# Gate loads of the first merge group in pairs, and the order of the last scan visit's products

## The chip, the cores and the metric

The kernel runs on one core of a Trainium2 chip. A core has a matrix engine (TensorE, PE in the profile), VectorE (DVE), ScalarE (ACT), GpSimd (POOL) and SyncE (SP), which here issues the DMA transfers between the chip's memory (HBM) and the on-chip buffer (SBUF). Products of PE go to a buffer of their own, PSUM. The metric is the device time of one execution in microseconds (us); lower is better.

## The reference

One layer of a diffusion backbone over 2048 latent tokens of width 1024, with 256 context tokens as a prefix. Two bidirectional linear-attention mixers, GLA and Gated DeltaNet (GDN), run on the same normalised input. What matters here is the merge of the two at the end:

```python
def branch_merge(oa, ob, ag, bg, mg, ...):
    ya = rmsnorm(oa, gla_onorm).reshape(b, t, GLA_V) * jax.nn.silu(ag)
    yb = rmsnorm(ob, gdn_onorm).reshape(b, t, GDN_V) * jax.nn.silu(bg)
    gates = jax.nn.sigmoid(mg + b_gate.astype(jnp.float32))
    merged = gates[..., :D_MODEL] * jnp.matmul(ya, w_gla_out) + gates[..., D_MODEL:] * jnp.matmul(yb, w_gdn_out)
    return jnp.matmul(merged, w_o)
```

The layer then adds `gt_x * out` to the input and applies a final RMSNorm. The mixers scan chunk by chunk in both directions, each scan from the final state of the context in that direction.

## The kernel before

The program is unrolled Python. A framework gives each tile a buffer, sets the waits and orders the instructions of each engine; where two instructions are ready, the one that comes first in the program goes first, and a buffer that comes free goes to the earliest one waiting for its pool. `keep_in_program_order` (`pin`) fixes the order of an instruction by hand.

Three phases follow each other: `phase_proj` (input projections, convolution, the in-chunk solves of GDN), `phase_mix` (the scans) and `phase_out` (merge and output projection).

`phase_mix` has 16 visits. In each, one 128-token chunk of the forward and one of the backward direction is scanned. Several generators are woven: `weave` always advances the one whose next step, at 1/n of its length per step, comes first. In a 17th round, `si == len(order)`, the last visit's products are still to be made: `gdn_scan` for both directions (weight 12) gives the products of L1055, L1066, L1077 and L1097, and `gla_end` (weight 4) gives the GLA output products L1346 and L1354 and their adds on VectorE, L1364. Beside them the merge is begun: `out_weights` and then `out_merge(0)` (weight 10).

`out_weights` loads the raw weights of both output projections, one block of 128 columns after the other (`out_raw`, L1559, 512 KB per block), and `split` makes a high part (ScalarE, L132) and a low part (L135, on VectorE for even blocks and GpSimd for odd ones). At its first step it also splits the first group's `y` (`out_y(0)`), whose raw tiles come by `y_raw` (L1580). It yields once, after block 0.

The raw tiles, of `out_raw`, `y_raw` and later of the rows of `w_o` and other reloads, all come from one pool with four buffers of 4 KB per partition (`self.rp`, name `wr`), opened in the last visit.

`out_merge(g)` merges one group of 512 tokens; `groups` has four. For each of eight column blocks j and for the two mixers i, it loads a gate tile `ga` (L1600, 128x512, 256 KB), makes twelve matmuls (L1605: four k times high-high, high-low and low-high) into a PSUM tile, and multiplies with the gate on VectorE (L1608). The two halves are added (L1612) and stored to `d_m` (L1613). In group 0 the gates have three small buffers (`os`), and both products use `pm`, which has two PSUM tiles. The half i = 0 reads the tiles `y0` and `y2`, the half i = 1 reads `y1` and `y3`.

`phase_out` begins with `out_y(1)`: `y_raw` for the four quarters of the second group, casts and low parts, into tiles of its own. Then, for g = 1 to 3, it calls `out_y(g + 1)` for the next group's `y` and runs `out_merge(g)` with other work woven in (`prep`: rows of `w_o`; `blocks`: splits of the last factors). The transposes L1416 with L1417 and the stores L1419 belong to the finishing of scanned chunks.

Of the kernel before, what the change touches and what calls it, by code (L numbers as in the profile page):

```python
# [11 lines left out]
F32 = mybir.dt.float32  # L12
# [10 lines left out]
P = 128  # L23
# [74 lines left out]
class Build:  # L98
# [1340 lines left out]
    def phase_mix(self):  # L1439
        nc = self.nc  # L1440
# [39 lines left out]
        for si in range(len(order) + 1):  # L1480
            gens = []
            if si == NLAT // 2:
                self.act_set("natural_log_exp_and_others")
            if si == len(order) - 1:
                self.rp = self.pool("owr", 4, side="right")
                self.raws = [self.out_raw(j) for j in range(2)]
                self.yraw = [self.y_raw(self.groups[0][0], hf) for hf in range(2)]
            if si == 1:
                self.ectx.close()
                gtc = gctx.enter_context(ExitStack())  # L1490
                gt = self.gt_row(gtc)
            if si in (1, 2):
                gens.append((itertools.islice(gt, 5 if si == 1 else 6), 6))
            elif si == 3:
                gtc.close()
            if si == 0:
                for d in range(2):
                    gens.append((itertools.chain(*[self.gdn_scan(p[d][1], False) for p in pairs]), 8))
                gens.append((self.gla_ctx_states(pairs), 4))
            else:  # L1500
                pair = [x[0] for x in prev]
                self.gla_prev(pair)
                for x in prev:
                    x[1]["prev"] = self.prev_o(1, x[1]["c"] - NCTX)
                for x in prev:
                    gens.append((self.gdn_scan(x[1], True, si == len(order)), 12))
                if si == len(order):
                    gens.append((self.gla_end(pair), 4))
            cur = []
            if si < len(order):  # L1510
                for d in range(2):
                    c = order[si][d]
                    a, b = ({"kp": kps[si % 2]} for _ in range(2))
                    self.gla_load(d, c, a)
                    cur.append((a, b))
                if si == 0:
                    rest()
                for d in range(2):
                    c, a = order[si][d], cur[d][0]
                    a["v"] = a["kp"].tile([P, 512], F32, name="av")  # L1520
                    nc.sync.dma_start(a["v"], self.d_av[c])
                for d in range(2):
                    self.gdn_load(d, order[si][d], cur[d][1])
                if si == 0:
                    nc.sync.dma_start(self.am.rearrange("p l t -> p (l t)"), self.io["ki"][:, 2 * len(MASK_LEVELS) * 64:])
                gens.append((self.gla_step(*[x[0] for x in cur], pair if si else None), 24))
            else:
                gctx.close()
                self.out_open()
                gens.append((itertools.chain(self.out_weights(), self.out_merge(0)), 10))  # L1530
            self.weave(gens)
            for g in self.fin:
                next(g)
            if si == len(order):
                self.fin_rest(4)
            prev = cur
# [25 lines left out]
    def out_weights(self):  # L1562
        raws = self.raws
        for j in range(8):
            cs = slice((j % 2) * P, (j % 2) * P + P)
            if j == 0:
                self.out_y(0)
            if j < 6:
                raws.append(self.out_raw(j + 2))
            hi, lo = self.wab[j // 2]  # L1570
            self.split(hi[:, :, cs], lo[:, :, cs], raws.pop(0), lo=self.LO[j % 2])
            if j == 0:
                yield

    LO = ("vector", "gpsimd")

# [16 lines left out]
    def out_merge(self, g):  # L1593
        nc, y = self.nc, self.y2
        pin = self.tc.keep_in_program_order if g else lambda x: x
        for j in range(8):
            gs = []
            for i in range(2):
                ga = (self.sp if i else self.spa).tile([P, 512], F32, name="ga")
                nc.sync.dma_start(ga, self.d_gate[g, :, 8 * i + j, :])  # L1600
                ps = self.pv() if g and i else self.pm.tile([P, 512], F32, name="pm")
                n = 0
                for k in range(4):
                    for wi, yy in ((0, y[i]), (0, y[2 + i]), (1, y[i])):
                        nc.tensor.matmul(ps, self.wab[j // 2][wi][:, 4 * i + k, (j % 2) * P:(j % 2) * P + P],  # L1605
                                         yy[:, k, :], start=(n == 0), stop=(n == 11))
                        n += 1
                pin(nc.vector.scalar_tensor_tensor(ga, ga, 1.0, ps, op0=ALU.add, op1=ALU.mult))  # L1608
                gs.append(ga)
                if i == 0:  # L1610
                    yield
            pin(nc.vector.tensor_tensor(gs[0], gs[0], gs[1], op=ALU.add))  # L1612
            nc.sync.dma_start(self.d_m[g, :, j, :], gs[0])  # L1613
            yield
# [284 lines left out]
```

## Time and profile before

| | |
|---|---|
| median of 3 runs | 2144.94 us (2143.9 to 2147.0) |
| the profiled execution | 2138.93 us |
| its span, first to last instruction | 2136.9 us |
| granted PE clock, mean | 0.987 |
| PE busy | 2041.9 us (96%) |
| VectorE, ScalarE, GpSimd busy | 1283.2, 914.5, 816.7 us |
| first product of group 0 (L1605) | 1779.3 us from the span's start |
| last L1605 of group 3 | 1970.3 us |

The profile gives one execution. Its timeline lists instructions by engine with start, duration, engine, line, operation, output and inputs; a bracket at the end is the time for which the engine was idle before, and what ended it. "x12" is a run of twelve instructions merged into one row, and the duration is that of the run. A matmul's end is modelled, so a row's duration is a little longer than the step from one to the next. SPq is the queue in which SP issues DMAs; its rows have the time of the issue, not of the transfer. A view by windows has, for each stretch of time, the busy time of every engine, PE's granted clock, the busy share of the DMA engines and GB/s.

### The profile page before, as it was taken

How to read it: one execution, taken by the hardware profiler on the slowest of the kernel's cores; microseconds unless marked ns; L12 is line 12 of the kernel's file. 1: busy time of each engine (PE TensorE's matmuls, PEld its weight loads, DVE VectorE, ACT ScalarE, POOL GpSimd, SP SyncE). 2: the span in 40 equal slices, each digit the busy share in tenths (PEclk: the TensorE clock that was granted, in tenths of full speed). 3: DMA queues.
4: the chain of work that ended last, by engine and by line, in shares of the span. 5: the costliest groups of instructions: out<-in, count | busy, mean ns of one | idle time of the engine just before them, and what ended most of it. 6: DMA issues, size and time to landing. Idle time of an engine off the chain costs nothing.

```text
span 2136.9 us, 40356 instructions
## 1 busy us (share of the span) xinstructions
PE 2041.9 (96%) x15208; PEld 1674.4 (78%) x15208; DVE 1283.2 (60%) x2229; ACT 914.5 (43%) x2208; POOL 816.7 (38%) x746
## 2 busy tenths in 40 slices
PE   6999999999999999999999999899988888999998
PEld 2688888888888888777777777688888876787786
DVE  2713555556667653555555655466567776576776
ACT  3645245555543223444344444345545656002332
POOL 2410122222221104566666665256556656002211
PEclk9999999999999999999999999999999999999999
DMA  8323122222222224443344443688888877898543
GB/s 285 111 86 119 48 58 76 63 62 65 73 63 72 72 72 133 149 143 129 122 146 141 159 144 110 202 306 284 296 291 297 296 250 233 286 317 300 181 147 111
DMA packets 272862, 346.96 MB, mean 162 GB/s; under 512 B 25000, under 2 KB 176796, under 8 KB 272668
## 3 DMA queue, kind: packets, MB, share of 16 engines
q1 hardware_dynamic: 272668, 344.39, 48.8%
q8 instruction: 120, 1.97, 0.4%
q14 instruction: 74, 0.61, 0.1%
HBM read 218.73 MB, written 125.57 MB: 161 GB/s over the span
## 4 chain that ended last, share of the span: by engine, by line
PE 72%; DMA 7%; issue 7%; DVE 6%; ACT 5%; POOL 3%; SPq 1%; DVEq 0%; POOLq 0%; ACTq 0%
PE pz L371 46%; PE pm L1605 3%; PE pz L1605 2%; DMA g<-dg 2%; PE pe L943 1%; PE pe L1125 1%; PE pl L1002 1%; PE pl L995 1%; PE pz L1087 1%; DMA ga<-dgate 1%; PE pl L1003 1%; DVE ql L1222 1%; ACT E L1216 1%; PE pp L1823 1%; PE pz L1066 1%
## 5 line engine op out<-in xcount | busy, mean ns | idle before, releaser
L371 PE MATMUL pz<-hi,wh 128*128 128x512 f32 (+1 forms) x1560 | 621.2, 399 | 1.1 <-DVE hi L134 1.1
L371 PE MATMUL pz<-lo,wh 128*128 128x512 f32 (+1 forms) x1560 | 600.1, 385 | 1.8 <-POOL lo L135 1.8
L371 PE MATMUL pz<-hi,wl 128*128 128x512 f32 (+1 forms) x1520 | 588.1, 387 | 0.0
L371 PEld LDWEIGHTS pz<-lo,wh 128*128 128x128 f32 x1560 | 294.6, 189 | 51.2 <-POOL lo L135 3.7
L371 PEld LDWEIGHTS pz<-hi,wh 128*128 128x128 f32 x1560 | 294.1, 189 | 47.1 <-DVE hi L134 1.7
L371 PEld LDWEIGHTS pz<-hi,wl 128*128 128x128 f32 x1520 | 285.9, 188 | 53.7 <-issue 0.4
L135 POOL TENSOR_TENSOR wl<-w,wh 128x1024 fp32r<-128x1024 f32 x44 | 109.6, 2491 | 437.5 <-ACT wh L132 314.2
L575 DVE SCALAR_TENSOR_TENSOR acc<-zpad,cw,acc 128x1024 f32<-128x1024 f32 x192 | 269.5, 1403 | 6.6
L880 DVE CAST_PREDICATED U<-kit,pl 128x256 f16<-128x256 int32 x216 | 91.3, 432 | 138.7 <-PE pl L1003 135.0
L996 ACT CAST ppb<-pl 128x256 f16<-128x256 f32 x216 | 73.8, 374 | 169.9 <-PE pl L995 163.2
L1605 PE MATMUL pm<-y,wb 128*128 128x512 f32 x480 | 118.5, 399 | 5.2 <-DVE ga L1608 2.9
L1223 POOL TENSOR_TENSOR E<-E,ak 128x256 f32<-128x256 f32 x96 | 79.4, 847 | 111.5 <-ACT E L1216 67.0
L135 DVE TENSOR_TENSOR sql<-sq,sqh 128x512 fp32r<-128x512 f32 (+1 forms) x36 | 28.0, 804 | 142.7 <-ACT sqh L132 142.5
L1605 PEld LDWEIGHTS pm<-y,wb 128*128 128x128 f32 x480 | 90.9, 191 | 26.9 <-DVE y L135 2.6
L630 POOL TENSOR_TENSOR acc<-acc,sq 128x512 f32<-128x512 f32 x32 | 50.6, 1590 | 138.7 <-ACT sq L629 90.9
L560 ACT COPY zpad<-pz 128x512 f32<-128x512 f32 x48 | 28.2, 588 | 137.5 <-PE pz L371 137.5
L1125 PE MATMUL pe<-wt,gh 128*128 128x256 f32 x264 | 77.0, 320 | 8.8 <-ACT E L1216 4.9
L880 DVE CAST_PREDICATED Tm<-kit,pl 128x256 f16<-128x256 int32 x180 | 76.4, 425 | 0.0
L1002 PEld LDWEIGHTS <-Tm 128*128 128x128 f16 x864 | 55.1, 98 | 26.5 <-issue 22.0
L132 ACT CAST wh<-w 128x1024 fp32r<-128x1024 f32 x44 | 46.2, 1049 | 68.6 <-PE pz L371 56.0
L1216 ACT ACTIVATE E<-pe 128x128 f32<-128x128 f32 x320 | 64.5, 306 | 18.7 <-PE pe L1125 18.1
L1222 DVE TENSOR_TENSOR ql<-E,q 128x256 f32<-128x256 f32 x96 | 64.1, 694 | 13.6 <-ACT E L1213 11.7
(326 smaller groups left out, 4265.3 us busy)
## 6 DMA issues: line engine op xcount, KB each, us to landing
gd<-dgd SPq DMA_DIRECT2D x32, 768.0 KB, 7.8
w<-in_w_in SPq DMA_DIRECT2D x44, 512.0 KB, 3.5
dgate<-ob SPq DMA_DIRECT2D x128, 128.0 KB, 1.8
qk<-dqkv SPq DMA_DIRECT2D x32, 512.0 KB, 5.9
ga<-dgate SPq DMA_DIRECT2D x64, 256.0 KB, 4.7
x<-in_x SPq DMA_DIRECT2D x28, 512.0 KB, 5.0
dqkv<-acc SPq DMA_DIRECT2D x192, 64.0 KB, 1.6
dgd<-tm SPq DMA_DIRECT2D x36, 256.0 KB, 2.5
```

The lines of the kernel that those rows point to most:

```text
L135: getattr(nc, lo).tensor_tensor(dst_lo, src, dst_hi.bitcast(F32), op=ALU.subtract)
L371: nc.tensor.matmul(ps[:, 0:n], a[:, kk, :], b[:, kk, :], start=(k == 0), stop=(k == last - 1))
L575: nc.vector.scalar_tensor_tensor(acc, src, wcol, acc, op0=ALU.mult, op1=ALU.add)
L630: nc.gpsimd.tensor_tensor(v, v, r, op=ALU.mult)
L880: self.nc.vector.copy_predicated(out, mv, data)
L996: nc.scalar.copy(ppl, pc.rearrange("p h (j i) -> p h j i", i=m))
L1002: nc.tensor.matmul(pu[:, h], Tm[:, h], ppl[:, h], start=True, stop=True)
L1125: self.nc.tensor.matmul(out, g[:, i, ct * P:(ct + 1) * P], self.wt[:, d, cols[0]:cols[1]], start=(j == 0), stop=(j == 1))
L1216: nc.scalar.activation(E[:, ct, li, x].rearrange("p (j e i) -> p e j i", e=2, i=m), s[:, x * P:(x + 1) * P].rearrange("p (e j i) -> p e j ...
L1222: nc.vector.tensor_tensor(ql[:, li], E[:, :, li, 0], q, op=ALU.mult)
L1223: nc.gpsimd.tensor_tensor(E[:, :, li, 1], E[:, :, li, 1], k, op=ALU.mult)
L1605: nc.tensor.matmul(ps, self.wab[j // 2][wi][:, 4 * i + k, (j % 2) * P:(j % 2) * P + P], yy[:, k, :], start=(n == 0), stop=(n == 11))
```

## The change

Three edits. `gla_end` gets weight 8 in place of 4, so its steps come at 1/8, 2/8 and 3/8 of the weave and not at 1/4, 2/4 and 3/4. `out_weights` yields three times after block 0, so weight blocks 1 to 7 and the first product come at 4/10 of the weave and not at 2/10; the products of `gdn_scan` have their steps at 1/12 to 5/12. And in group 0, for the blocks j = 1 to 7, both gate tiles of a block come in one transfer of 512 KB into a tile of the pool `wr`; block 0 keeps the two small tiles, and the other groups are as before.

```diff
                 if si == len(order):
-                    gens.append((self.gla_end(pair), 4))
+                    gens.append((self.gla_end(pair), 8))
...
             if j == 0:
                 yield
+                yield
+                yield
...
         for j in range(8):
             gs = []
+            if g == 0 and j:
+                t = self.w_raw().rearrange("p (i n) -> p i n", i=2)
+                nc.sync.dma_start(t, self.d_gate[g, :, j:16:8, :])
             for i in range(2):
-                ga = (self.sp if i else self.spa).tile([P, 512], F32, name="ga")
-                nc.sync.dma_start(ga, self.d_gate[g, :, 8 * i + j, :])
+                if g == 0 and j:
+                    ga = t[:, i]
+                else:
+                    ga = (self.sp if i else self.spa).tile([P, 512], F32, name="ga")
+                    nc.sync.dma_start(ga, self.d_gate[g, :, 8 * i + j, :])
```

`w_raw` takes a tile of the pool `wr`:

```python
    def w_raw(self):
        return self.rp.tile([P, 8, P], F32, name="wr").rearrange("p a b -> p (a b)")
```

## The prediction

> **What bounds the kernel now.** I read the page first, for the share of PE, then the chain of work that ended last around the first merge group, then each engine's timeline there. I write block j for the eight column blocks of a merge group and call its two products GLA (i = 0) and GDN (i = 1).
>
> ```profile
> span 2136.9 us, 40356 instructions
> PE 2041.9 (96%) x15208; PEld 1674.4 (78%) x15208; DVE 1283.2 (60%) x2229; ACT 914.5 (43%) x2208; POOL 816.7 (38%) x746
> ```
>
> PE is busy for 96% of the span, and no edit removes a matmul. Only idle PE time or a low clock can be won. Inside the first group the chain steps through loads of the gate tile `ga`, and VectorE's timeline shows waits for them:
>
> ```profile
> 1814.20 0.69 DVE L1608 SCALAR_TENSOR_TENSOR ga<-ga,pm 128x512 f32<-128x512 f32 x1 [1.90 <-DMA ga<-dgate]
> ...
> 1829.20 0.69 DVE L1608 SCALAR_TENSOR_TENSOR ga<-ga,pm 128x512 f32<-128x512 f32 x1 [3.11 <-DMA ga<-dgate]
> ```
>
> The columns are start, duration, engine and line; the bracket is the idle time before and what ended it. VectorE waits up to 3.11 us for a gate load. What matters is PE's own timeline:
>
> ```profile
> 1774.05 2.12 PE L1077 MATMUL pz<-rhs,gd 128*128 128x128 f32 x14
> 1778.67 0.66 PE L1416 MATMUL pe<-kf,og 128*128 128x128 f32 x4 [2.49 <-POOL og L1412]
> ...
> 1779.30 0.48 PE L1605 MATMUL pm<-y,wb 128*128 128x512 f32 x1
> 1782.07 5.06 PE L1605 MATMUL pm<-y,wb 128*128 128x512 f32 x11 [2.29 <-DVE y L135]
> 1786.93 1.16 PE L1346 MATMUL pz<-av,at 128*128 128x128 f32 x8
> 1788.02 1.10 PE L1354 MATMUL pz<-Sa,q 64*64 64x128 f32 x32
> 1789.05 3.02 PE L1605 MATMUL pm<-y,wb 128*128 128x512 f32 x12
> 1791.91 1.95 PE L1097 MATMUL pz<-vn,gd 128*128 128x128 f32 x16
> 1793.61 16.87 PE L1605 MATMUL pm<-y,wb 128*128 128x512 f32 x72
> 1812.44 16.60 PE L1605 MATMUL pm<-y,wb 128*128 128x512 f32 x72 [1.96 <-DVE ga L1608]
> 1830.03 5.69 PE L1605 MATMUL pm<-y,wb 128*128 128x512 f32 x24 [0.99 <-DVE ga L1608]
> 1835.57 1.03 PE L1416 MATMUL pe<-kf,oi 128*128 128x128 f32 x8
> ...
> 1840.18 2.96 PE L1605 MATMUL pz<-y,wb 128*128 128x512 f32 x12
> ```
>
> The reader should see two separate losses. Ahead of the first product PE is idle for 2.49 us and 2.29 us, and then 11 matmuls take 5.06 us, where 72 later take 16.87, that is 0.234 us each: 2.49 us more than 11 x 0.234. Inside the group the gate loads cost PE just 1.96 + 0.99 = 2.95 us, since two PSUM tiles let it run ahead of VectorE. All of it is 4.78 + 2.49 + 2.95 = 10.2 us, or 0.48% of the span: the ceiling. About 0.2% (4.3 us) is what a measurement of this kernel can tell from no change.
>
> **The change part by part.**
>
> *Scan products ahead of the first product.* `gla_end` and the empty yields put L1346 and L1354 (1786.93 to 1789.05, about 2.1 us) and L1097 (1.78 us from 1791.91 up to 1793.61, roughly) ahead of L1605 in program order. The GLA part needs only states and the masked score tile, finished long before, so it can lie in the idle time. Nothing is added: the same instructions, no DMA. VectorE's adds behind them (L1364, L1098) move with them, past the splits of weight blocks 2 and 4; I cost that at nothing, since VectorE is busy for only 1.19 and 0.73 of 2 us from 1784 to 1788 (rows below). Without that cover it would be one add, some 0.7 us, on pair 1's load. Block 1 could then begin about 2 to 4 us sooner than 1793.61, and some of the half-clock stretch may go too. But I cost this edit by what is late next, and that is the load of block 1's gates.
>
> *Gate pairs in the weight buffers.* Seven pairs replace 14 single loads (512 KB instead of two of 256 KB; the bytes are equal; SP issues 7 fewer DMAs of some 0.4 us). Before, block 1's GLA gate was loaded at 1761.40 with block 0's two, in the third small buffer (first row below). Now the first pair needs one of four `wr` buffers, and those hold raw weights until their splits end:
>
> ```profile
> 1761.40 1.82 SPq L1600 DMA_DIRECT2D ga<-dgate  x3
> ...
> 1786.07 0.51 SPq L1559 DMA_DIRECT2D wr<-in_w_gla_out  x1
> 1790.38 1.22 DVE L135 TENSOR_TENSOR wb<-wr,wb 128x1024 fp32r<-128x1024 f32 x1
> 1791.43 2.40 POOL L135 TENSOR_TENSOR wb<-wr,wb 128x1024 fp32r<-128x1024 f32 x1 [1.16 <-ACT wb L132]
> 1794.90 1.21 DVE L135 TENSOR_TENSOR wb<-wr,wb 128x1024 fp32r<-128x1024 f32 x1
> 1796.43 2.40 POOL L135 TENSOR_TENSOR wb<-wr,wb 128x1024 fp32r<-128x1024 f32 x1 [2.61 <-ACT wb L132]
> 1791.98 1.05 ACT L132 CAST wb<-wr 128x1024 fp32r<-128x1024 f32 x1 [0.63 <-DMA wr<-in_w_gdn_out]
> ```
>
> Weight blocks 4 to 7 give their buffers back at 1790.38 + 1.22 = 1791.6, 1793.8, 1796.1 and 1798.8. A load of 512 KB took, from issue to the cast that waited for it, 1786.07 to 1791.98 = 5.9 us; a row below has 4.2. So pair 1 lands between 1795.8 and 1797.5; I take 1796.5. Block 2's first product needs the PSUM tile that VectorE frees 0.69 us later: about 1797.3. Before, it began at 1793.61 + 24 x 0.234 = 1799.2. From there pairs 2 to 7 are early by several us, both gate waits go, and PE runs 6 x 24 x 0.234 = 33.7 us to 1831.0. Before, the group ended at 1830.03 + 5.69 = 1835.7. That is a **gain of 4.7 us** (3.7 to 5.4) inside the group, for both edits together.
>
> *What this moves.* Those buffers aren't empty in the trace. They hold the raw `y` of the second group:
>
> ```profile
> 1797.97 1.74 SPq L1580 DMA_DIRECT2D wr<-dy  x4
> ...
> 1806.46 0.85 SPq L1580 DMA_DIRECT2D wr<-dy  x2
> 1810.68 1.05 ACT L132 CAST y<-wr 128x1024 fp32r<-128x1024 f32 x1 [1.67 <-DMA wr<-dy]
> 1811.80 2.38 POOL L135 TENSOR_TENSOR y<-wr,y 128x1024 fp32r<-128x1024 f32 x1 [1.19 <-ACT y L132]
> ```
>
> Here the four raw tiles load from 1797.97 on, and the last is split by 1814.2, some 21 us before group 1 needs it. In the change the seven pairs come first in program order, and each holds its buffer until its merged block is stored. Pairs 5, 6 and 7 take what blocks 1, 2 and 3 release; the four `y` loads get what blocks 4, 5, 6 and 7 release. The last waits for the end of the group. The store that it waits for, and the SP load released by it:
>
> ```profile
> 1800.08 0.69 DVE L1612 TENSOR_TENSOR ga<-ga 128x512 f32<-128x512 f32 x1
> 1800.80 0.32 SPq L1613 DMA_DIRECT2D dm<-ga  x1
> 1809.74 0.32 SPq L1613 DMA_DIRECT2D dm<-ga  x1
> 1812.05 0.32 SPq L1600 DMA_DIRECT2D ga<-dgate  x1
> 1815.64 0.32 SPq L1613 DMA_DIRECT2D dm<-ga  x1
> 1818.29 0.32 SPq L1600 DMA_DIRECT2D ga<-dgate  x1
> ```
>
> From the end of a block's last product to its store is about 1.5 us (0.69 + 0.69 and handovers); the store lands after 2.31 (1809.74 to 1812.05) or 2.65 us (1815.64 to 1818.29). I take 2.6. A `y` load took 1806.46 to 1810.68 = 4.2 us beside other traffic; with little else in flight I take 3.8, near the middle between 4.2 and 3.2 (a store's 2.31 and 0.85 of issue); the far end is the 5.9 of a weight load. Then ScalarE casts (1.05 us), and VectorE (1.22) or GpSimd (2.40) makes the low part. For the GDN half, released by block 7: 1831.0 + 1.5 + 2.6 + 3.8 + 1.05 + 2.40 = 1842.4. Group 1's second product began at 1840.18 before, so it is **2.2 us late**. For the GLA half, released by block 6 (5.6 us sooner, faster low part): 1835.6. So PE idles from 1831.0 to 1835.6, less about 2.1 us of transposes (L1416: 8 take 1.03 us in the row at 1835.57, and 16 are left) that fit in, works until 1838.4, and idles again until 1842.4. Queued behind on ScalarE and GpSimd are the casts of group 2's `y`, wanted only 45 us later: they cost nothing. On SP the weight loads for `w_o` come later by some us, with a whole group's time to spare.
>
> *The clock.* The rows of the first stage, by 2 us (the number before the DMA share is the granted clock):
>
> ```profile
> 1768.00:1770.00 2.00, 1.02 (x9) 1.02 (x10) 2.00 (x9) 1.90 (x12) 1.80 (x3) 1.00 0.03 8
> 1770.00:1772.00 2.00, 2.00 (x12) 2.00 (x11) 1.71 (x6) 1.96 (x11) 1.61 (x2) 0.52 0.00 0
> ...
> 1780.00:1782.00 2.00, 0.00 (x0) 0.00 (x0) 2.00 (x6) 1.04 (x1) 1.73 (x2) 0.58 0.69 199
> 1784.00:1786.00 2.00, 2.00 (x6) 1.60 (x5) 1.19 (x1) 0.78 (x1) 0.26 (x1) 0.50 1.11 309
> 1786.00:1788.00 2.00, 2.00 (x11) 1.62 (x9) 0.73 (x2) 1.04 (x1) 0.12 (x1) 0.72 1.12 283
> ...
> 1830.00:1832.00 2.00, 1.97 (x9) 1.67 (x10) 0.86 (x2) 0.00 (x0) 0.00 (x0) 1.00 0.28 80
> ```
>
> Full clock turns to half after two gaps of 2.49 and 2.29 us, and already once around 1770 after smaller ones. The new gaps, 2.5 and about 4 us, are longer, so I expect a fall. If it comes in the first gap, it mostly slows a product that would wait anyway: nothing. In the second it costs up to 2.5 us, as above. I take 0.8, nearer to nothing, since the first gap comes first.
>
> The Trainium skill, "TensorE: Matmul & The Clock Gate", Part 1, says that the clock is halved after an idle window of about 3.4 us that runs freely. By that alone the first gap would be harmless and the second would halve the clock only where a window falls wholly inside it. The rows around 1770 and 1780 speak against so strict a reading, since no single gap there is that long.
>
> *Sum.* 2.2 + 0.8 = +3.0 us after the second group's second product; from there on PE is busy without a gap until the next stage, so nothing absorbs it. The profiled execution took 2138.93 us; the median of the runs is 2144.94, 6.0 us more. I add the difference to the median: **2147.9 us**, +0.14%. The bounds of the unknown durations: early ends (pair 1 at 1795.8, store 2.3, load 3.2, no clock price) give 3.0 - 0.7 - 0.3 - 0.6 - 0.8 = +0.6; late ends (+1.0, +0.1, +2.1, clock +1.7) give +7.9, hardly all at once.
>
> **The rivals.**
>
> *A. Clock stays full* in the gaps. The rest as forecast: +2.2, 2147.1 us. For it: after the gap of 0.99 us that ends at 1830.03 the row at 1830 has 1.00; against it, the rows near 1780. This is the case by the strict rule of the page named above. Chance 0.13.
>
> *B. Slower: the second gap grows and halves the clock.* If `y` loads take 5.9 us, as weight loads did, the GDN half comes 2.1 us later, and a gap of 6 us surely costs the full 2.5: 2.2 + 2.1 + 2.5 = +6.8, 2151.7 us. It decides from a load of about 5 us. For it: group 1's gate loads start in the same microseconds. Against: in the row at 1830 the DMA engines are busy for 0.28 only. Chance 0.25.
>
> *C. Faster: `y` isn't held back*, because buffers are given out in another order. Then group 1 follows at once and the gain of 4.7 us stays: 2140.2 us, and up to 2 us better if the early stage also keeps full clock and pair 1 comes early. For it: `y` loads have no other cause to wait. Against: the raw loads in the trace of before stand in program order. Chance 0.17.
>
> *D. The scan products don't move* ahead in effect (PSUM tiles `pz` are three, and the scan's own products hold them). Then block 2 begins at 1799.2 as before, 2 us later than in the forecast: +5.0, 2149.9 us. Chance 0.05.
>
> **How the numbers follow.** The forecast has 0.40, and its own range is about +0.6 to +5. C is the only faster case, 0.17. Slower are B and D, 0.30. Within 0.2% are the forecast and A, 0.53. The range, 2140 to 2152 us, goes from C's value to just above B's, and leaves out the far ends of both.
>
> **What would show it.** In the changed trace: L1354 ahead of the first L1605; no wait of VectorE for gates after block 2; the last L1580 load of group 1's `y` issued only after the store (L1613) of block 7; PE idle in two places around the border of groups 0 and 1, ended by `y` low parts; and a granted clock below 1 there. I am wrong if the `y` loads are issued before 1815, or if PE goes from group 0 to group 1 without a gap.

## The result and the profile after

The changed kernel took 2162.41 us (median of five runs, 2160.95 to 2169.06) where the kernel before, timed beside it, took 2144.42 (median of six); a sixth run of the changed kernel, 7337.84 us at a mean granted clock of 0.26, is left out here and in the ratio. The ratio is 1.0097 (95% interval 1.0077 to 1.0118): about 20.8 us **slower**, outside the range that was given. All times "in us" below that come from a ratio are the ratio's excess times 2144.4.

The profiled execution has a longer span, with the same number of matmuls:

```profile
span 2164.1 us, 40346 instructions
PE 2052.4 (95%) x15208; PEld 1680.6 (78%) x15208; DVE 1289.4 (60%) x2229; ACT 913.8 (42%) x2208; POOL 820.0 (38%) x746
```

Two profiled executions differ already ahead of the change, so I count from a common mark: the last L1354 row of the scan visit before the 17th round. These are the mark, the first product of the last stage (L1823 before, L1831 after) and the product there that follows the first pass, all from PE's timeline, before:

```profile
1760.18 1.10 PE L1354 MATMUL pz<-Sa,q 64*64 64x128 f32 x32
1970.53 0.63 PE L1823 MATMUL pz<-y,hi 128*128 128x512 f32 x2
1989.63 0.70 PE L1823 MATMUL pz<-y,hi 128*128 128x512 f32 x2 [1.77 <-DVE x L1830]
```

and after, with what lies between (L1613 is the old L1605; L1616, L1620 and L1621 are the old L1608, L1612 and L1613; L1608 is the old L1600):

```profile
1764.41 1.10 PE L1354 MATMUL pz<-Sa,q 64*64 64x128 f32 x32
...
1775.50 2.08 PE L1346 MATMUL pz<-av,at 128*128 128x128 f32 x8 [1.68 <-ACT at L1252]
...
1785.86 0.47 PE L1613 MATMUL pm<-y,wb 128*128 128x512 f32 x1
1788.78 2.50 PE L1613 MATMUL pm<-y,wb 128*128 128x512 f32 x5 [2.45 <-DVE y L135]
1792.64 3.70 PE L1613 MATMUL pm<-y,wb 128*128 128x512 f32 x11
...
1807.14 30.20 PE L1613 MATMUL pm<-y,wb 128*128 128x512 f32 x132 [1.14 <-DVE wr L1616]
1839.53 3.02 PE L1613 MATMUL pm<-y,wb 128*128 128x512 f32 x12 [2.18 <-DVE wr L1616]
...
1845.80 4.38 PE L1613 MATMUL pm<-y,wb 128*128 128x512 f32 x11 [0.77 <-DVE y L135]
1851.94 2.83 PE L1613 MATMUL pz<-y,wb 128*128 128x512 f32 x11 [1.53 <-POOL y L135]
...
1880.51 4.35 PE L1613 MATMUL pm<-y,wb 128*128 128x512 f32 x12 [2.64 <-DVE ga L1616]
...
1985.36 4.61 PE L1613 MATMUL pm<-y,wb 128*128 128x512 f32 x12 [2.77 <-DVE ga L1616]
...
1992.61 0.63 PE L1831 MATMUL pz<-y,hi 128*128 128x512 f32 x2
...
1999.72 0.79 PE L1831 MATMUL pz<-y,lo 128*128 128x512 f32 x1 [3.68 <-DVE lo L1652]
...
2016.86 0.70 PE L1831 MATMUL pz<-y,hi 128*128 128x512 f32 x2 [1.93 <-DVE x L1838]
```

Measured from the mark, and with the rows of before that the prediction shows:

| point | before | after | lost so far |
|---|---|---|---|
| first product of group 0 | 19.1 | 21.5 | +2.3 |
| first product of block 2 | 39.0 | 42.7 | +3.7 |
| end of group 0 | 75.5 | 78.1 | +2.6 |
| end of group 1's second product | 83.0 | 90.4 | +7.4 |
| first product of the last stage | 210.4 | 228.2 | +17.8 |
| the product after its first pass | 229.4 | 252.4 | +23.0 |
| end of the span | 376.7 | 399.7 | +23.0 |

So four pieces: +2.6 us up to the end of group 0 (where a gain of 4.7 was forecast), +4.8 at the border, +10.4 in the rest of groups 1 to 3 (where PE was forecast to run without a gap), +5.2 in the first pass of the last stage. After that nothing moves. Of the 10.4, three gaps of PE are 6.4 (2.64, 2.77 and one of 1.00 at 1926.64) and two falls of the clock, below, 3.1. The reader should see that gaps ended by `ga` (VectorE's gate product) have appeared at 1880.51 and 1985.36, far behind the group that was edited, and one ended by `lo` at 1999.72.

**Why the first group gains nothing.** ScalarE's timeline of after has the cast of weight block 4 behind a square (L1409) that waits for a scan output, and SP's queue has the first pair only after it:

```profile
1798.05 0.31 ACT L1409 ACTIVATE fsq<-oi 128x128 bf16<-128x128 f32 x1 [5.54 <-DVE oi L1098]
...
1798.36 1.03 ACT L132 CAST wb<-wr 128x1024 fp32r<-128x1024 f32 x1
```

```profile
1801.63 0.61 SPq L1602 DMA_DIRECT2D wr<-dgate  x1
...
1826.81 0.60 SPq L1608 DMA_DIRECT2D ga<-dgate  x1
...
1837.16 2.54 SPq L1582 DMA_DIRECT2D wr<-dy  x4
1840.22 0.32 SPq L1621 DMA_DIRECT2D dm<-wr  x1
1844.39 2.22 SPq L1582 DMA_DIRECT2D wr<-dy  x5
...
1862.03 0.42 SPq L1608 DMA_DIRECT2D ga<-dgate  x1
```

The prediction gave the first `wr` buffer back at 1791.6, which is 31.4 us behind the mark; the pair was issued 37.2 us behind it. But the square is the smaller part of these 5.8 us. The load of weight block 4 was itself late, 26.9 us behind the mark where before it was 22.0. The issue of its GLA half, before and after:

```profile
1782.14 0.49 SPq L1559 DMA_DIRECT2D wr<-in_w_gla_out  x1
```

```profile
1791.28 0.41 SPq L1559 DMA_DIRECT2D wr<-in_w_gla_out  x1
```

The cast then came 5.6 us late (before it began at 1788.50). In SP's order the load stands behind a store (L1419, 1790.19) that waited for VectorE. The rows of L1582, the loads of raw `y`, stand between the stores L1621, as was forecast.

**Where the gates went.** The same rows hold a trap. SP issues a gate load at 1826.81 and the next one at 1862.03: none for 35 us. But by 1826.81 eight loads had been issued, two for block 0 and six for group 1, and its six small buffers were full; before, they were full only at 1843.4. The seventh load needs VectorE's first sum of group 1 and follows it at once (that sum ends at 1861.6). So it is VectorE that is late. Its first gate product of group 1, before:

```profile
1841.78 0.68 DVE L1608 SCALAR_TENSOR_TENSOR ga<-ga,pm 128x512 f32<-128x512 f32 x1
```

and after, behind a low part of group 2's `y` (group 1's four casts are over by 1849.5):

```profile
1857.53 2.17 DVE L135 TENSOR_TENSOR y<-wr,y 128x1024 fp32r<-128x1024 f32 x1 [4.43 <-ACT y L132]
1859.62 0.68 DVE L1616 SCALAR_TENSOR_TENSOR ga<-ga,pm 128x512 f32<-128x512 f32 x1
```

That is 81.6 and 95.2 us behind the mark, 13.6 us late, where PE's second product ends 7.4 us late. The view of waits for groups 1 to 3 (engine, line, what it waited for: total us, times, longest) has VectorE's waits for gates, before (1832 to 1992):

```profile
DVE ga L1608 <- DMA ga<-dgate: 7.3, 4, 2.5
```

and after (1840 to 2020) these, and PE's for VectorE's gate product, which before had none:

```profile
DVE ga L1616 <- DMA ga<-dgate: 35.6, 13, 5.6
...
PE pm L1613 <- DVE ga L1616: 6.4, 3, 2.8
```

Only the second of these rows is lost time: while PE runs ahead, a wait of VectorE costs nothing. The order of the weave alone (below) has 31.1 us of such waits of VectorE and 2.3 of PE's (1836 to 2020).

SP waits for VectorE's sums (to store them; 43.8 us in this window, 14.5 before), VectorE waits for gates, and the gates stand behind SP's waits: a ring in which a delay can be handed on from block to block. The start of the last stage shows one turn of it. SP's queue, then VectorE:

```profile
1988.59 4.32 SPq L1708 DMA_DIRECT2D wr<-dwoB  x2
...
1993.50 0.97 SPq L1608 DMA_DIRECT2D ga<-dgate  x2
```

```profile
1998.38 0.69 DVE L1616 SCALAR_TENSOR_TENSOR ga<-ga,pm 128x512 f32<-128x512 f32 x1 [5.27 <-DMA ga<-dgate]
1998.98 1.29 DVE L1652 TENSOR_TENSOR lo<-r,hi 128x512 fp32r<-128x512 f32 x2
```

SP is held for 4.32 us by two reloads into `wr` that wait for buffers; the last gates of group 3 are issued behind them at 1993.50; VectorE stands 5.27 us for them; `lo`, which the last stage needs, stands behind that product in VectorE's order; and PE's row at 1999.72 is idle for 3.68 us. The rest of the 5.2 us there, about 1.5, is the clock, which was 0.57 from 1999 to 2003. VectorE's order did the same inside the border: the second gate product of block 6, behind the low part of `y`, is what PE waited for in the row at 1839.53 (2.18 us):

```profile
1837.65 1.23 DVE L135 TENSOR_TENSOR y<-wr,y 128x1024 fp32r<-128x1024 f32 x1 [5.02 <-ACT y L132]
1838.79 0.68 DVE L1616 SCALAR_TENSOR_TENSOR wr<-wr,pm 128x512 f32<-128x512 f32 x1
```

**The clock** fell as feared, and again later. By windows (length, then PE's and the others' busy time, then the granted clock, DMA share and GB/s), after:

```profile
1843.00:1850.00 7.00, 5.22 (x17) 3.84 (x16) 4.40 (x6) 2.09 (x2) 1.83 (x2) 0.76 0.62 191
...
1878.00:1888.00 10.00, 7.49 (x27) 6.01 (x28) 7.26 (x11) 0.00 (x0) 0.00 (x0) 0.83 0.84 291
...
1985.00:1993.00 8.00, 7.64 (x26) 6.12 (x27) 7.62 (x10) 3.65 (x5) 3.30 (x1) 0.79 0.84 292
```

Before, it was 1.00 from 1836 to 1990. Twelve products took 4.35 and 4.61 us at 1880.51 and 1985.36, against 2.96 elsewhere.

### The profile page after: what moved, and what is told of

The parts are those of the page before. It is cut to its first block, busy times and chain, and to the rows that moved or that the text cites. A ratio compares the mean times of both kernels' runs of the same rounds, so it can differ in the third digit from the quotient of the medians.

```text
span 2164.1 us, 40346 instructions
## 1 busy us (share of the span) xinstructions
PE 2052.4 (95%) x15208; PEld 1680.6 (78%) x15208; DVE 1289.4 (60%) x2229; ACT 913.8 (42%) x2208; POOL 820.0 (38%) x746
## 4 chain that ended last, share of the span: by engine, by line
PE 67%; DMA 9%; issue 7%; DVE 7%; ACT 5%; POOL 3%; SPq 1%; DVEq 0%; POOLq 0%; ACTq 0%
PE pz L371 45%; DMA g<-dg 2%; PE pm L1613 2%; PE pe L943 1%; PE pe L1125 1%; DMA ga<-dgate 1%; PE pl L1002 1%; PE pl L995 1%; PE pl L1003 1%; PE pz L1087 1%; DVE ql L1222 1%; DVE acc L575 1%; PE pp L1831 1%; ACT E L1216 1%; DMA av<-dav 1%
## 5 line engine op out<-in xcount | busy, mean ns | idle before, releaser
L1613 PE MATMUL pm<-y,wb 128*128 128x512 f32 x480 | 123.2, 410 | 14.1 <-DVE ga L1616 6.4
L1613 PEld LDWEIGHTS pm<-y,wb 128*128 128x128 f32 x480 | 93.9, 198 | 38.0 <-DVE ga L1616 8.2
```

## The experiments

All run kernels are compared with the kernel before on the same chip. L numbers shift by a few lines between them; `ga` in a bracket (`wr` for a pair) is always the gate product and `y` a low part of `y`.

### Each edit by itself

The order of the weave alone (no pairs):

```diff
-                    gens.append((self.gla_end(pair), 4))
+                    gens.append((self.gla_end(pair), 8))
...
                 yield
+                yield
+                yield
```

> The order edit alone (gla_end weight 8, two more empty yields); gates in the three small buffers as before. Theory T (the whole loss comes from the raw y of groups 1 and 2, which wait for the weight buffers that the gate pairs hold): between 2140 and 2149 us, within 5 us of before, and no PE gap at the border of groups 0 and 1. Rival O (the new order costs it: ScalarE takes the squares of the last scan output ahead of the casts of weight blocks 4 to 7, as the changed trace shows at 1792 to 1798): 2154 us or more, over 10 us above before.

> Both halves of the order edit and no pairs, a second time with more rounds. If the halves cost only together: a ratio of 1.002 to 1.003 again. If the two are harmless as each was alone: 0.999 to 1.001, and the first run was high by chance.

Measured: 1.0024 (1.0009 to 1.0039), and the second time 1.0028 (1.0014 to 1.0042): 5 to 6 us slower, so not chance. The pairs alone, with the old order:

```diff
+            if g == 0 and j:
+                t = self.w_raw().rearrange("p (i n) -> p i n", i=2)
+                nc.sync.dma_start(t, self.d_gate[g, :, j:16:8, :])
...
-                ga = (self.sp if i else self.spa).tile([P, 512], F32, name="ga")
-                nc.sync.dma_start(ga, self.d_gate[g, :, 8 * i + j, :])
+                if g == 0 and j:
+                    ga = t[:, i]
+                else:
+                    ga = (self.sp if i else self.spa).tile([P, 512], F32, name="ga")
+                    nc.sync.dma_start(ga, self.d_gate[g, :, 8 * i + j, :])
```

> The gate pairs alone, the weave as before. Theory T: 2157 to 2166 us, 13 to 22 us above before, with y loads of group 1 issued only after stores of blocks 4 to 7 and PE gaps at the border of groups 0 and 1. Rival O: at most 8 us above before, 2152 us.

Measured: 1.0070 (1.0045 to 1.0095), 15.0 us slower. The two parts together make 20 to 21 us, the whole of it. PE's timeline of the pairs alone has the gaps of after, with the same enders:

```profile
1832.65 3.02 PE L1611 MATMUL pm<-y,wb 128*128 128x512 f32 x12 [2.59 <-DVE wr L1614]
...
1844.80 2.83 PE L1611 MATMUL pz<-y,wb 128*128 128x512 f32 x11 [1.66 <-POOL y L135]
...
1991.56 0.80 PE L1829 MATMUL pz<-y,lo 128*128 128x512 f32 x1 [5.24 <-DVE lo L1650]
```

### Is it the hold on group 1's `y`?

Three pairs only, so that one of the four buffers goes to `y` at once and the others after the pairs of blocks 1 to 3:

```diff
-            if g == 0 and j:
+            if g == 0 and 0 < j < 4:
...
-                if g == 0 and j:
+                if g == 0 and 0 < j < 4:
```

> The whole change, but pairs only for blocks 1 to 3; blocks 4 to 7 take the small buffers. The fourth weight buffer then goes to y at once, and the others after blocks 1 to 3. Theory T: 2142 to 2152 us, most of the loss gone, y loads of group 1 from about 1800 to 1820 us of the span. Rival O: still 2155 us or more.

> Pairs for blocks 1 to 3 alone, the weave as before. If pairs in the buffers that are truly empty save the gate gaps of group 0 (2.95 us) and the order edit costs 5 us: 2137 to 2142 us, 1 to 4 us below before. If e4 came out level only because pairs make the order edit harmless: 2141 to 2146 us.

Measured with the new order: 0.9996 (0.9983 to 1.0009); with the old order: 0.9988 (0.9973 to 1.0002). The cost is gone in both. But fewer pairs change the loads of group 0 as well, so a second test keeps all seven and frees `y` from the pool: group 1's raw `y` is loaded straight into the tile of its low part and split in place.

```diff
-                raw = self.yraw.pop(0) if self.yraw else self.y_raw(self.groups[g][e], hf)
+                if g != 1:
+                    raw = self.yraw.pop(0) if self.yraw else self.y_raw(self.groups[g][e], hf)
...
+                if g == 1:
+                    b = self.groups[g][e]
+                    for x in range(2):
+                        self.nc.sync.dma_start(dst[1][:, :, x].bitcast(F32), self.d_y[2 * b + x, :, 4 * hf:4 * hf + 4, :])
+                    raw = dst[1].bitcast(F32)
```

> The whole change, but the raw y of group 1 is loaded straight into its low-part tile and split in place, so it needs no weight buffer; the pairs keep all seven. If the waiting y causes all the loss that e1 (order alone) doesn't have: about 5 us above before, 2145 to 2150 us, and no PE gap at the border of groups 0 and 1. If only the border (7.6 us in the changed trace) hangs on it and the late gate loads of groups 1 to 3 have a cause of their own: 2152 to 2158 us.

> Seven pairs, the weave as before, y of group 1 loaded in place (no weight buffer). If the hold on y is all that is wrong with the pairs: 2137 to 2144 us. If the pairs cost by themselves: 2150 us or more, near e2.

Measured with the whole change: 1.0031 (1.0013 to 1.0050), 6.6 us slower in place of 20.8; with the pairs and the old order: 1.0012 (0.9991 to 1.0033), 2.6 us in place of 15.0. So the wait of group 1's `y` for `wr` buffers carries 12 to 14 us, and what is left in the first is about the order edit's 5 to 6. Without the wait, the first product of the last stage comes at 212.0 us from the mark (the mark is at 1763.20 in that run; 210.4 before, 228.2 after), so most of the loss in groups 1 to 3 went too, though only the source of that `y` was changed: it is a consequence of that wait. VectorE's waits for gates stayed; it is PE's waits for VectorE that nearly went (1836 to 2020):

```profile
DVE ga L1622 <- DMA ga<-dgate: 33.3, 14, 6.3
...
PE pm L1619 <- DVE ga L1622: 1.9, 2, 1.2
```

VectorE's first gate product of group 1 begins at 82.5 us from the mark in this run, nearly as early as before.

### What hands the delay on

First I held that group 2's `y`, whose low parts VectorE makes in the middle of group 1's gate products, was what delayed the gates. So group 2's `y` was asked for five steps later:

```diff
-                    y = self.y2
-                    self.out_y(g + 1)
-                    nxt, self.y2 = self.y2, y
...
-                for _ in gen:
+                for n, _ in enumerate(gen):
+                    if g < 3 and n == (5 if g == 1 else 0):
+                        self.out_y(g + 1)
+                        nxt = self.y2
```

> The whole change, but the y of group 2 is asked for only after five steps of group 1's merge, so that its low parts don't stand ahead of group 1's gate products on VectorE. If the waits on VectorE behind group 2's y carry the second part of the loss (all that comes after group 1's second product, about 15 us in the changed trace): 2148 to 2156 us. If the loss after the border comes from late gate loads of another cause, or from the border alone: within 3 us of the change, 2160 to 2167 us.

Measured: 1.0105 (1.0081 to 1.0128). Nothing was won, so what the theory forecast **failed**. But the run doesn't refute it, since the edit put another hold in place of the first. VectorE's first gate product of group 1 was on time (80.2 us from the mark, which is at 1764.86 there). Now group 2's `y` loads, the last at 1869.43, stood in SP's queue just ahead of the gates, whose next loads came 105.5 us from the mark (before 86.5, after 97.6):

```profile
1870.35 1.37 SPq L1608 DMA_DIRECT2D ga<-dgate  x3
```

The run also shows that late loads of `w_o` aren't needed for the loss: they were issued 76.9 us from the mark there, near 75.2 before, and not 91.6 as in after. The next suspect was SP's order, where gate loads stand behind stores that wait for VectorE. The stores of groups 1 to 3 were moved to GpSimd's queue:

```diff
-            nc.sync.dma_start(self.d_m[g, :, j, :], gs[0])
+            (nc.gpsimd if g else nc.sync).dma_start(self.d_m[g, :, j, :], gs[0])
```

> The whole change, but the merged blocks of groups 1 to 3 are stored from GpSimd's queue, so that SP's queue has no store ahead of a gate load. The border stays as in the change. If gate loads in groups 1 to 3 are late because they stand behind stores in SP's queue: 5 to 12 us below the change, 2150 to 2158 us, and VectorE's waits for gates fall from 35.6 us to under 15. If they are late for their buffers or for DMA: within 3 us of the change, 2160 us or more.

Measured: 1.0067 (1.0043 to 1.0090), 14.4 us slower, so about 6.4 of the 20.8 are won back, though the two intervals overlap by a little (1.0077 to 1.0090). VectorE's waits for gates fall to these (under 15 was expected), in the same view and the window 1836 to 2020:

```profile
DVE ga L1616 <- DMA ga<-dgate: 22.5, 11, 5.2
```

Inside groups 1 to 3 one gap is left, 1.21 us, where after had 2.64, 1.00 and 2.77; the border's gaps, which the stores don't cause, remain, and so does `lo` (3.70 us); one of 2.21 us for a cast is new at the start of the last stage. So the stores in SP's order carry a part of the delay, clearly in PE's gaps and less surely in the time. How the rest is shared between VectorE's order and SP's stays open. For the reloads in SP's order (the row at 1988.59) no run of its own was made: that part is read from the trace.

### What is dear in the order edit

> Only the part of the weave edit that raises the weight of the last scan products (gla_end 8), without the two empty steps ahead of block 3's and block 4's weight casts. Theory (the empty steps cost: ScalarE's casts of blocks 4 to 7 fall behind the squares of the last scan output, so the gate gaps of group 0 grow from 2.95 us to 6): 2139 to 2144 us, within 2 us of before, and the gate gaps of group 0 stay at 2 to 4 us. Rival (the moved scan products themselves cost): 2145 us or more, with the gaps of the first experiment.

> Only the two empty steps, without the raised weight of the scan products. Theory (the empty steps cost): 2145 to 2149 us, gate gaps in group 0 of 5 to 6 us. Rival (the moved scan products cost): 2140 to 2144 us, gaps near 3 us.

The raised weight alone measured 0.9990 (0.9974 to 1.0006), the empty steps alone 1.0008 (0.9996 to 1.0020). My theory, that the empty steps cost because they put ScalarE's casts behind the squares, **fell** too. They do put the cast of block 4 there, as ScalarE's timeline of the empty steps alone shows:

```profile
1786.46 0.31 ACT L1409 ACTIVATE fsq<-oi 128x128 bf16<-128x128 f32 x1 [2.01 <-DVE oi L1098]
...
1786.77 1.03 ACT L132 CAST wb<-wr 128x1024 fp32r<-128x1024 f32 x1
```

The raised weight alone does it to the cast of block 5 (before, it was block 7's). Either costs nothing that can be measured: without pairs no gate load needs the buffers that those splits free. With pairs one does:

```diff
-                    gens.append((self.gla_end(pair), 4))
+                    gens.append((self.gla_end(pair), 8))
```

> All seven pairs and the raised weight, without the empty steps. If the empty steps make the whole change dearer than the pairs alone: 1.006 to 1.008, as the pairs alone (1.0070). If the raised weight does, because ScalarE's weight casts of blocks 4 to 7 then stand between the squares of the last scan output: 1.009 to 1.010, as the whole change.

> Pairs for blocks 1 to 3 and the raised weight of the scan products, without the empty steps. If moving the scan products earlier is worth what block 2's start gains: below 0.998. If the raised weight is harmless and useless, as alone (0.999): 0.998 to 1.000, as three pairs alone.

All seven pairs with the raised weight: 1.0093 (1.0063 to 1.0123), against 1.0070 without it; three pairs with it: 1.0014 (0.9998 to 1.0031), against 0.9984 without it (below). The first pair is issued 35.6 us behind the mark with all pairs and the raised weight (mark at 1760.71), 31.6 with all pairs in the old order (mark at 1760.82). SP's rows of the two:

```profile
1796.30 6.43 SPq L1600 DMA_DIRECT2D wr<-dgate  x4
```

```profile
1792.42 1.12 SPq L1600 DMA_DIRECT2D wr<-dgate  x1
```

In the run with the raised weight it isn't a square that holds the pair back. The cast of block 4 ran at 1791.47, ahead of the squares, but VectorE made the low part behind an add of the scan (L1098) that waited for PE:

```profile
1793.85 0.69 DVE L1098 TENSOR_TENSOR oi<-pz,oi 128x512 f32<-128x512 f32 x1 [0.44 <-PE pz L1097]
...
1795.05 1.22 DVE L135 TENSOR_TENSOR wb<-wr,wb 128x1024 fp32r<-128x1024 f32 x1
```

With the old order that low part began at 1791.18 and the pair could go at 1792.42. For the seven pairs the two intervals overlap, so a cost in time isn't shown; for the three they don't, except by a little with a first measurement of three pairs (0.9973 to 1.0002, above). What remains **open**: why the two halves of the order edit, each harmless without pairs, cost 5 to 6 us together without pairs, and nothing with three pairs (0.9996, above). The first run of the two has wider gate gaps in group 0, four of 1.87, 1.71, 1.43 and 1.13 us, against 1.96 and 0.99 us before. In the second run five gaps of 2.84 us in all stand there, no more than before, and 2.57 us at the last stage's `lo`. The place of the loss differs from run to run, so I name no mechanism.

### The fastest version

> Pairs for blocks 1 to 3 only, group 1's raw y straight into its low-part tile, the order of the weave as before. If a wait for group 1's y still costs after three pairs: 2134 to 2138 us, below three pairs alone (2139.2). If three pairs already leave y free: 2138 to 2142 us, as three pairs alone.

> Pairs for blocks 1 to 3 only with the order of the weave as before, a second time with more rounds. If it really gains what the first product of block 2 gains: a ratio of 0.997 to 0.999 with an interval below 1. If the gain of the first time was chance: 0.999 to 1.001.

Three pairs with group 1's `y` loaded directly measured 0.9994 (0.9979 to 1.0009), no better than three pairs alone: `y` no longer limits. Three pairs alone, a second time: 0.9984 (0.9974 to 0.9995), 2136.5 us beside 2139.97 for the kernel before. It is the only version with an interval below 1, by 3.4 us. The gate waits of group 0 nearly go: PE's gaps there are 0.44 and 0.32 us.

## Why the prediction was wrong

- **What bounds the kernel**, and the ceiling of 10 us that could be won: right as far as these runs go. The best version won 3.4.
- **VectorE's adds, "I cost that at nothing", and "what is late next", the load of block 1's gates**: the second was right. The step that failed in group 0 is the time at which weight block 4 gives its buffer back. The sum took 1791.6 over from the trace of before, though the change puts weight blocks 1 to 7 later in the program. It came 5.8 us later from the mark: 4.9 by the block's own load, the rest behind it on ScalarE and VectorE. Where the raised weight was run with the pairs, it was VectorE's add that held the low part back, so that nothing was too little as well. Block 2, which waits for pair 1's gate product, began 3.7 us late in place of 1.9 early. The half clock of the rows from 1775.50 to 1792.64 (11 products in 3.70 us, 5 in 2.50) lies ahead of that wait.
- **The gain of 4.7 us inside group 0**: not there; the group ended 2.6 us late. That is 7.3 us of the error: 3.7 + 1.9 = 5.6 by the start of block 2, and the rest by a gap the forecast didn't have, the 2.18 us at 1839.53, offset in part by products that were a little shorter than the 0.234 us of the sum (132 in 30.20 us). The gate waits did go, as forecast.
- **`y` held back until the stores of blocks 4 to 7**: the mechanism was right, in its order and with its gaps ended by ScalarE's cast, VectorE's and GpSimd's low parts. Rival C was wrong. The border itself cost 4.8 us behind the end of group 0, where the forecast had 6.9 (4.7 + 2.2) plus 0.8 for the clock: if anything less.
- **The casts of group 2's `y` "cost nothing", the weight loads for `w_o` have "a whole group's time to spare", and so "from there on PE is busy without a gap until the next stage"**: the step that failed for the rest. Behind the border the sum put nothing; the trace has +10.4 us in groups 1 to 3 and +5.2 in the first pass of the last stage. It asked when group 2's `y` and `w_o` are wanted, and not what stands behind them in the orders of VectorE and SP: group 1's gate products, 13.6 us late, and the gate loads that need their buffers. With group 1's `y` taken out of the pool nearly all that is lost up to the last stage is won back (212.0 us in place of 228.2; 210.4 before). How it is shared between the two orders is read from traces: group 2's `y` moved later won nothing, as its loads then stood ahead of the gates in SP's order, and the stores moved off SP won about 6.4 of 20.8.
- **Clock price 0.8 us at the border**: there it is 4.38 us for 11 products in place of 11 x 0.234 = 2.6, so 1.8 us; and two more falls, 4.35 and 4.61 against 2.96 us, cost 1.4 and 1.7. The fall in the last stage is within the 5.2.

Point by point the error sums up: 7.3 in group 0, 4.8 - 7.7 = -2.9 at the border, 10.4 and 5.2 behind it, 20.0 us together, which is the profile's loss of 23.0 less the forecast's 3.0.

The Trainium skill, "TensorE: Matmul & The Clock Gate", Part 1, which the prediction weighed, puts the return to half clock at an idle window of about 3.4 us. The runs halve it after single gaps of 2.64 and 2.77 us, so no window of that length was wholly idle; here page and measurement differ.

## What to carry to other kernels

When a prefetch borrows buffers of a shared pool, list who took them before, and then follow each engine and queue that handles *that* work in order: what stands behind it is late too, whether it needs the pool or not. In this kernel such a wait is priced by the tightest work behind it (gate tiles, one per 2.8 us of PE), not by the load that waits. Count what the bottleneck itself waits for: VectorE's waits for gates were 35.6 us in the change and 33.3 with `y` out of the pool, but PE's were 6.4 and 1.9. Borrow only as many buffers as the next user leaves idle: three pairs won 3.4 us where seven lost 15.

## What the runs showed of the hardware

The granted clock doesn't go by the length of a gap alone. In all seven pairs with the raised weight, 12 products took 3.06 us after an idle time of 2.89 us, and 4.60 after one of 2.14:

```profile
1874.61 3.06 PE L1611 MATMUL pm<-y,wb 128*128 128x512 f32 x12 [2.89 <-DVE ga L1614]
...
1978.30 4.60 PE L1611 MATMUL pm<-y,wb 128*128 128x512 f32 x12 [2.14 <-DVE ga L1614]
```

So an estimate for a gap of 2 to 3 us has two values here, nothing or about 1.5 us, and these runs don't tell ahead which.
